# Layer 0 of a two-layer decoder trunk: queries and keys projected ahead of values and gates, and one head's attention laid over both projections of the next

## The chip, the cores and the metric

The kernel runs on one core of a Trainium2 chip. The metric is the device time of one execution in microseconds (us), and of several executions the median. The engines are named as in the profile: PE is TensorE's matmul side and PEld its weight loads, DVE is VectorE, ACT is ScalarE, POOL is GpSimd, and SP is the queue from which nearly all DMAs are issued.

## The reference

The model has two layers over 512 positions of width 2048 in float32. Layer 0 is differential attention with 8 heads, layer 1 is forgetting attention with 16 heads over keys and values that are projected once between the layers. Only the inside of layer 0 is changed:

```python
def diff_attention(h, w_in, w_out, ...):          # h = x * (1 + scale) + shift
    q, k, v, g = jnp.split(h @ w_in, 4, axis=-1)  # q, k: 8 heads x 2 x 128; v, g: 8 heads x 256
    ...
    sc = einsum('bqhcd,bkhcd->bhcqk', qb, k) + bias      # two score maps c per head, causal, ALiBi
    p = softmax(sc)
    a = p[:, :, 0] - lam * p[:, :, 1]
    o = einsum('bhqk,bkhe->bqhe', a, v)
    o = rms_norm(o, subln_g) * (1.0 - lam_init) * silu(g)
    return o @ w_out
```

The shift, scale and gate of both layers and of the shared keys and values are products of one vector (`silu(c)`) with large weight matrices (`w_mod`, `kv_w_mod`).

## The kernel before, in words

Every float32 product is made of three fp32r matmuls (function `products`, lines L173, L174, L175): each operand is split into a high part (a cast on ACT) and a low part (a subtraction on DVE). 512 positions are four blocks of 128; the width is 16 blocks of 128.

A projection is a `group`: four accumulator banks, 8 weight tiles ("subs") of 256 rows by 512 columns, and for each sub one burst for each bank. A burst is 2 x 3 matmuls of 128x512, so that a group is 32 bursts and 192 matmuls. The weight tiles come through `WeightStream`: a load on SP's queue (`wst`, four buffers), a cast on ACT (`whi`, L93) and a subtraction on DVE (`wlo`, L94), made two subs ahead of their use. The order of the weight tiles is written out once, in `ws.order`.

Head h of layer 0 has two groups. `vg[h]` projects its values and gates (the activations are the stationary operand; in the trace `acc<-whi,hh`), `qk[h]` its two queries and two keys (the weights are stationary; `acc<-hh,whi`). After its last burst a bank is evacuated: `evac_vg` splits the values and makes the gate, `evac_qk` splits a query or a key (L656, L657, L168, L169). The first two heads are projected mostly in the stage before, the last bank of their keys in a small group `kk`.

Attention of a head is a list of pieces, and after each burst (`tick`) one piece is popped and issued. For the four blocks i of positions and the two score maps there are `score` (three matmuls into `sc`, a DVE instruction that adds the bias and takes the minimum, L699, the exponential on ACT, L703, and DVE instructions that combine the two maps), `turn` (transposes into the one `tr` bank, L720, then a split into `ah`, `al`), `values` (products into `o`; after every second block `norm`, the RMS norm: squares on ACT, L749, a reciprocal root of 12 small DVE instructions, L750 and L246 to L255, and two multiplications with the gate, L753) and `store` (two transposes of the result, L767, which wait for L753, and a scaled copy into `ogT`, L769). `None` is a burst without a piece. `drain()` issues all pieces that are left.

Beside the bursts runs `background`: the products of `silu(c)` with `w_mod` and `kv_w_mod`, 256 steps of one DVE instruction (L384 or L386, `macc<-ms`) each, with a 512 KB load (`ms`, two buffers) for every two steps, and one short PE, DVE and DMA sequence after each sixteen steps (`mod_row`, L406 to L409). The argument `bg` of a group says in which bursts a step is taken: `k % 2` gives 16 steps in a group, `k % 3 > 0` gives 21. After the last head the out-projection takes a step in every burst until the steps are used up.

The order before: `kk`, `vg[2]` beside the attention of head 0, `qk[2]` beside that of head 1, and for h = 3 to 7 first `vg[h]` beside the attention of head h-1, then `qk[h]` beside no attention. In `qk[7]`, `split_og` (through `early`) also splits the finished heads' results into the operands of the out-projection, 14 casts on ACT and 14 subtractions on DVE. The attention of head 7 runs beside the first group of the out-projection. Instructions of an engine run in the order in which they stand; that order is made from the order of the program by a scheduler that may move independent instructions past each other.

Of the kernel before, what the change touches and what calls it, by code (L numbers as in the profile page):

```python
# [20 lines left out]
A_HEADS = 8  # L21
# [88 lines left out]
def tile_yoco(  # L110
# [147 lines left out]
    ws = WeightStream(nc, wpool)  # L258
    vg = [Job(a_w_in, [(4096 + 256 * h, 256), (6144 + 256 * h, 256)]) for h in range(A_HEADS)]
    qk = [Job(a_w_in, [(256 * h, 256), (2048 + 256 * h, 256)]) for h in range(A_HEADS)]  # L260

    first = {h: (Job(a_w_in, [(256 * h, 256), (2048 + 256 * h, 128)]), vg[h]) for h in range(2)}
# [16 lines left out]
                ws.add(j, s)  # L279
    ws.add_job(kk)  # L280
    for h in range(2, A_HEADS):
        ws.add_job(vg[h])
        ws.add_job(qk[h])
    for j in [o[1] for o in oA] + vj + kj + bj + [o[1] for o in oB]:
        ws.add_job(j)

    pieces = []
# [18 lines left out]
    def group(job, natural, evac, banks=range(4), bg=0, before_sub=None, after_sub=None, hold=0, after_held=None):  # L306


        acc = {b: acc_bank() for b in banks}
        w = job.width  # L310
        count = 0
        ns = KT // 2

        def burst(s, b, hi, lo):
            nonlocal count
            for kk in range(2):
                kt = 2 * s + kk
                bs = slice(b * P, (b + 1) * P)
                start, stop = kt == 0, kt == KT - 1
                if natural:  # L320
                    products(acc[b][:, :w], (Hh[kt][:, bs], Hl[kt][:, bs]), (hi[kk][:, :w], lo[kk][:, :w]), start, stop)
                else:
                    products(acc[b], (hi[kk][:, bs], lo[kk][:, bs]), (Hh[kt], Hl[kt]), start, stop)
            if s == ns - 1:
                evac(b, acc[b])
            tick(bg(count) if callable(bg) else bg)
            count += 1

        for s in range(ns - hold):
# [86 lines left out]
    part = {}  # L416
    with tc.tile_pool(name="start", bufs=2, reuse_waits="tile") as sp, tc.manual_schedule(engines={ET.DVE}):
# [110 lines left out]
        acc = {}  # L528
# [43 lines left out]
        def turn():  # L572
            lower()
            columns()
            while sum(sets[at["set"] - 1]) <= at["kt"]:
                sums()
                columns()
            turned.append((at["kt"], turn_x(at["kt"])))
            at["kt"] += 1
# [70 lines left out]
    def evac_qk(h):  # L650
        def fn(b, acc):
            name = ("q0", "q1", "k0", "k1")[b]
            hi = ap.tile([P, T], F32R, name=name + "h", tag=name + "h")
            lo = ap.tile([P, T], F32R, name=name + "l", tag=name + "l")
            if b < 2:
                S.activation(hi, acc, AF.Copy, scale=QS)  # L656
                V.scalar_tensor_tensor(lo, acc, QS, hi.bitcast(F32), op0=ALU.mult, op1=ALU.subtract)  # L657
            else:
                split(hi, lo, acc)
            cur[h, name] = (hi, lo)  # L660
        return fn

    def evac_vg(h):
        def fn(b, acc):
            if b == 0:
                cur[h, "v"] = (
                    ap.tile([P, TB, 256], F32R, name="vh", tag="vh"),
                    ap.tile([P, TB, 256], F32R, name="vl", tag="vl"),
                )
                cur[h, "sg"] = ap.tile([P, TB, 256], F32, name="sg", tag="sg")  # L670
            vh, vl = cur[h, "v"]
            split(vh[:, b, :], vl[:, b, :], acc[:, 0:256])
            th = ap.tile([P, 256], F32, name="th", tag="th", bufs=2)
            S.activation(th, acc[:, 256:512], AF.Tanh, scale=0.5)
            V.scalar_tensor_tensor(cur[h, "sg"][:, b, :], th, 1.0, acc[:, 256:512], op0=ALU.add, op1=ALU.mult)
        return fn

    def attention_a(h, lead=3, late=()):
        st = {}
        slope = 2.0 ** (-8.0 * (h + 1) / A_HEADS)  # L680

# [77 lines left out]
        def store(i):  # L759
# [11 lines left out]
                    )  # L771
            return fn

        return [
            *[None] * lead, score(0, 0), *late[0:1], score(0, 1), *late[1:2], score(1, 0), *late[2:3], score(1, 1), *late[3:4],
            turn(0), score(2, 0), values(0), turn(1), score(2, 1), values(1), score(3, 0), turn(2), score(3, 1), None,
# [3 lines left out]
    def drain():  # L780
        while pieces:
            tick(0)

    def first_qk(h):
        return [lambda b=b: evac_qk(h)(b, part[h][4 + b]) for b in (0, 2, 1)]

    def first_vg(h, src):
        return [lambda b=b: evac_vg(h)(b, src[b]) for b in range(4)]

    load_parameters()  # L790
    raw = {}

    def keep(key, acc):
        raw[key] = kpool.tile([P, T], F32, name="raw", tag="K")
        S.copy(raw[key], acc)
# [6 lines left out]
    def split_og(kts):  # L802
        for kt in kts:
            new_h(kt)
            split(Hh[kt], Hl[kt], ogT[kt])
# [2 lines left out]
    drain()  # L808
    pieces.append(lambda_columns)
    pieces.extend(attention_a(0, 2))  # L810
    group(vg[2], True, lambda b, acc: keep(b, acc), bg=lambda k: k % 2)
    drain()
    for h in range(2, A_HEADS):
        if h == 2:
            pieces.extend(first_qk(1))
            pieces.append(lambda: evac_qk(1)(3, raw["k1"]))
            pieces.extend(attention_a(1, 2, first_vg(1, part[1])))
        else:
            late = first_vg(2, raw) if h == 3 else ()
            pieces.extend(attention_a(h - 1, 3, late))  # L820
            group(vg[h], True, evac_vg(h), bg=lambda k: k % 2)
            drain()

        def early(s):
            if s >= 1:
                split_og((2 * s - 2, 2 * s - 1))

        def evac(b, acc, h=h):
            if b == 0:
                drain()  # L830
            evac_qk(h)(b, acc)

        group(qk[h], False, evac, bg=lambda k: k % 3 > 0, after_sub=early if h == A_HEADS - 1 else None)
    def ktile(name):
        return kpool.tile([P, T], F32, name=name, tag="K")

# [118 lines left out]
    npool, n, nstats = zp  # L955
# [81 lines left out]
    acc = [acc_bank() for _ in range(TB)]  # L1037
# [34 lines left out]
    for g in range(4):  # L1072
        if g == 2:
# [3 lines left out]
            after_sub=(lambda s: build_h((2 * s - 2, 2 * s - 1), ab["b"]) if s >= 1 else None) if g == 3 else None,  # L1077
# [221 lines left out]
```

## Time and profile before

| | |
|---|---|
| median of 3 runs | 2016.12 us (2012.25 to 2016.65) |
| the profiled execution's own time | 2017.03 us |
| its span, from the first to the last instruction | 2015.2 us |
| PE busy | 1966.7 us |
| DVE busy | 1334.4 us |
| ACT busy | 722.3 us |
| mean granted TensorE clock | 0.995 |

The page gives busy time by engine, the share of each engine in 40 slices, DMA queues, the chain of work that ended last, and groups of instructions. Behind it are views that answer for a stretch of time: busy time by engine and stretch ("windows"), instructions in order of time ("timeline"), and who waited for whom ("waits"). In the windows a row is the stretch in us, its length, then for PE, PEld, DVE, ACT and POOL the busy time and the number of instructions, then the granted clock, the busy share of the DMA engines and GB/s.

In the profiled execution the groups that the change touches stand at these times: `vg[2]` 222.0 to 278.8, `qk[2]` to 333.4, `vg[3]` to 388.3, `qk[3]` to 432.9, `vg[4]` to 486.8, `qk[4]` to 530.8, `vg[5]` to 587.2, `qk[5]` to 631.2, `vg[6]` to 685.9, `qk[6]` to 730.4, `vg[7]` to 784.3, `qk[7]` to 829.1, and then the out-projection.

### The profile page before, as it was taken

The numbers are of one execution on the slowest core, as the hardware profiler recorded it, in microseconds if no ns is written. First come the engines' busy times: TensorE is split into PE (matmuls) and PEld (weight loads), VectorE is DVE, ScalarE is ACT, GpSimd is POOL, SyncE is SP. The second block draws the span as 40 slices with busy tenths as digits, with TensorE's granted clock in tenths as the row PEclk, the third lists the DMA queues.
The fourth block names the chain that finished last, engine by engine and source line by source line (L and its number), as shares of the span: only waits on it lengthen the run. The fifth ranks groups of instructions, "written<-read, shape, count | busy, mean of one in ns | idle before, by whom it ended". The sixth has DMA issues, their size and how long they took to land.

```text
span 2015.2 us, 25053 instructions
## 1 busy us (share of the span) xinstructions
PE 1966.7 (98%) x9115; PEld 1624.6 (81%) x9115; DVE 1334.4 (66%) x2435; ACT 722.3 (36%) x1230; POOL 2.2 (0%) x10
## 2 busy tenths in 40 slices
PE   5999999999999999999999999999999999999997
PEld 4888878888878888888878877888888888888885
DVE  7887878777667677753575666645455555576678
ACT  2423444433333334432273222224333333453232
POOL 0000000000000000000000000000000000000000
PEclk8999999999999999999999999999999999999998
DMA  9995755574556565552344878844233323333754
GB/s 342 346 314 149 238 174 162 166 222 156 190 166 210 160 225 178 162 165 94 115 144 135 268 252 260 259 123 129 90 104 95 104 90 104 95 117 93 259 191 177
DMA packets 263095, 353.79 MB, mean 176 GB/s; under 512 B 18022, under 2 KB 162556, under 8 KB 262204
## 3 DMA queue, kind: packets, MB, share of 16 engines
q1 hardware_dynamic: 260592, 347.99, 53.7%
q10 hardware_dynamic: 2380, 4.21, 0.6%
q8 instruction: 71, 1.16, 0.2%
q14 instruction: 52, 0.43, 0.1%
HBM read 339.47 MB, written 12.66 MB: 175 GB/s over the span
## 4 chain that ended last, share of the span: by engine, by line
PE 77%; DVE 10%; DMA 10%; issue 2%; ACT 1%; SPq 1%; DVEq 0%; ACTq 0%
PE acc L173 22%; PE acc L175 22%; PE acc L174 22%; DMA ms<-in_w_mod_dram 7%; DVE macc L386 3%; DVE wlo L94 2%; PE sc L173 2%; PE sc L174 2%; PE sc L175 1%; DMA ms<-in_kv_w_mod_dram 1%; PE o L175 1%; PE o L174 1%; PE o L173 1%; PE tr L1163 1%; DMA sms<-in_w_mod_dram 1%
## 5 line engine op out<-in xcount | busy, mean ns | idle before, releaser
L93 ACT CAST whi<-wst 128x1024 fp32r<-128x1024 f32 (+2 forms) x339 | 349.5, 1032 | 672.9 <-PE acc L175 281.6
L94 DVE TENSOR_TENSOR wlo<-wst,whi 128x1024 fp32r<-128x1024 f32 (+2 forms) x339 | 404.4, 1195 | 268.1 <-ACT whi L93 263.9
L173 PE MATMUL acc<-whi,hh 128*128 128x512 f32 x1252 | 492.6, 397 | 0.9 <-ACT hh L933 0.8
L174 PE MATMUL acc<-wlo,hh 128*128 128x512 f32 x1252 | 489.7, 391 | 2.6 <-DVE wlo L94 2.6
L175 PE MATMUL acc<-whi,hl 128*128 128x512 f32 x1252 | 488.1, 390 | 0.0
L173 PE MATMUL acc<-hh,whi 128*128 128x512 f32 x1184 | 468.5, 396 | 1.3 <-ACT vt L977 0.9
L175 PE MATMUL acc<-hh,wlo 128*128 128x512 f32 x1184 | 462.3, 390 | 2.0 <-DVE wlo L94 2.0
L174 PE MATMUL acc<-hl,whi 128*128 128x512 f32 x1184 | 461.7, 390 | 0.0
L386 DVE SCALAR_TENSOR_TENSOR macc<-ms,cact,macc 128x512 f32<-128x512 f32 x360 | 269.9, 750 | 128.4 <-DMA ms<-in_w_mod_dram 95.6
L175 PEld LDWEIGHTS acc<-whi,hl 128*128 128x128 f32 x1252 | 235.3, 188 | 50.8 <-DVE hl L934 0.3
L174 PEld LDWEIGHTS acc<-wlo,hh 128*128 128x128 f32 x1252 | 235.6, 188 | 47.8 <-DVE wlo L94 4.3
L173 PEld LDWEIGHTS acc<-whi,hh 128*128 128x128 f32 x1252 | 235.7, 188 | 46.8 <-ACT hh L933 1.2
L175 PEld LDWEIGHTS acc<-hh,wlo 128*128 128x128 f32 x1184 | 222.3, 188 | 52.2 <-DVE wlo L94 4.2
L173 PEld LDWEIGHTS acc<-hh,whi 128*128 128x128 f32 x1184 | 222.5, 188 | 45.7 <-ACT vt L977 1.7
L174 PEld LDWEIGHTS acc<-hl,whi 128*128 128x128 f32 x1184 | 222.6, 188 | 41.1
L476 DVE SCALAR_TENSOR_TENSOR sacc<-sms,cact,sacc 128x512 f32<-128x512 f32 (+1 forms) x127 | 89.5, 705 | 4.8 <-DMA sms<-in_w_mod_dram 1.2
L1152 ACT ACTIVATE eb<-eb,mnb 128x128 f32<-128x128 f32 (+1 forms) x64 | 36.1, 563 | 96.4 <-DVE mnb L1149 95.2
L703 ACT ACTIVATE e<-e,mn 128x128 f32<-128x128 f32 (+3 forms) x64 | 36.0, 563 | 89.5 <-DVE mn L699 88.7
L1149 DVE CUSTOM_DVE_ANT_0 eb<-sc,biasb 128x128 f32<-128x128 f32 (+1 forms) x64 | 31.3, 490 | 52.7 <-PE sc L175 52.7
L1167 DVE TENSOR_TENSOR pTl<-tr,pTh 128x128 fp32r<-128x128 f32 (+1 forms) x64 | 31.2, 487 | 26.5 <-ACT pTh L1166 26.2
L1166 ACT CAST pTh<-tr 128x128 fp32r<-128x128 f32 (+1 forms) x64 | 27.2, 424 | 43.6 <-PE tr L1163 43.1
L769 ACT ACTIVATE ogT<-tr,subg 128x128 f32<-128x128 f32 x64 | 20.0, 364 | 56.4 <-PE tr L767 56.4
(251 smaller groups left out, 1739.2 us busy)
## 6 DMA issues: line engine op xcount, KB each, us to landing
wst<-in_a_w_in_dram SPq DMA_DIRECT2D x240, 256.0 KB
ms<-in_w_mod_dram SPq DMA_DIRECT2D x64, 512.0 KB
ms<-in_kv_w_mod_dram SPq DMA_DIRECT2D x64, 512.0 KB
wst<-in_kv_w_dram SPq DMA_DIRECT2D x64, 512.0 KB
ms<-in_w_mod_dram SPq DMA_DIRECT2D x128, 256.0 KB
wst<-in_b_w_in_dram SPq DMA_DIRECT2D x128, 256.0 KB
sms<-in_w_mod_dram SPq DMA_DIRECT2D x56, 512.0 KB
wst<-in_b_w_out_dram SPq DMA_DIRECT2D x48, 512.0 KB
```

The source lines that it names most:

```text
L93: self.nc.scalar.copy(hi[:, :, :w], st[:, :, :w])
L94: self.nc.vector.tensor_tensor(lo[:, :, :w], st[:, :, :w], hi[:, :, :w].bitcast(F32), op=ALU.subtract)
L173: PE.matmul(dst, lhs[0], rhs[0], start=start, stop=False)
L174: PE.matmul(dst, lhs[0], rhs[1], start=False, stop=False)
L175: PE.matmul(dst, lhs[1], rhs[0], start=False, stop=stop)
L386: V.scalar_tensor_tensor(acc, w, cact[:, kt : kt + 1], acc, op0=ALU.mult, op1=ALU.add)
L476: V.scalar_tensor_tensor(acc, w, sc, acc, op0=ALU.mult, op1=ALU.add)
L703: S.activation(e[:, :w], e[:, :w], AF.Exp, bias=mn, scale=-1.0, accum_out=rs)
L1149: V.tensor_tensor_reduce(out=e[:, :w], in0=sc[:, :w], in1=bias[:, :w], scale=-1.0, scalar=3.0e38, op0=ALU.add, op1=ALU.min, accum_out=mn)
L1152: S.activation(e[:, :w], e[:, :w], AF.Exp, bias=mn, scale=-1.0, accum_out=rs)
L1166: S.copy(pTh[:, 0 : i + 1, ts], src)
L1167: V.tensor_tensor(pTl[:, 0 : i + 1, ts], src, pTh[:, 0 : i + 1, ts].bitcast(F32), op=ALU.subtract)
```

## The change

`qk[h]` comes ahead of `vg[h]`, in the order of the weight tiles and in the order of the groups. The attention of heads 2 to 6 is cut into two lists: `first` (all scores, three of four `turn`s, two of four `values`, 22 places behind four empty ones) runs beside `qk[h]` of the next head, and `rest` (two `values`, the last `turn`, the four `store`s) beside `vg[h]`. The attention of head 0 now runs beside `qk[2]`, which takes no background steps; that of head 1 beside `vg[2]`, with 16. From head 3 on both groups take 21 steps. `qk[2]` is copied out of its banks (`raw`) and split later, beside `qk[3]`. The splitting of finished results (`early`) moves from `qk[7]` to `vg[7]`.

```diff
     for h in range(2, A_HEADS):
+        ws.add_job(qk[h])
         ws.add_job(vg[h])
-        ws.add_job(qk[h])
...
-    def attention_a(h, lead=3, late=()):
+    def attention_a(h, lead=3, late=(), spread=False):
...
+        if spread:
+            first = [
+                score(0, 0), None, score(0, 1), None, score(1, 0), None, score(1, 1), None, turn(0), None, score(2, 0), values(0),
+                None, turn(1), score(2, 1), None, values(1), score(3, 0), None, turn(2), None, score(3, 1),
+            ]
+            rest = [values(2), None, store(0), None, store(1), None, turn(3), None, None, values(3), *[None] * 9, store(2), None, store(3)]
+            return first, rest
         return [
...
-    group(vg[2], True, lambda b, acc: keep(b, acc), bg=lambda k: k % 2)
+    group(qk[2], False, lambda b, acc: keep(("qk", b), acc))
     drain()
-    for h in range(2, A_HEADS):
-        if h == 2:
-            pieces.extend(first_qk(1))
-            pieces.append(lambda: evac_qk(1)(3, raw["k1"]))
-            pieces.extend(attention_a(1, 2, first_vg(1, part[1])))
-        else:
-            late = first_vg(2, raw) if h == 3 else ()
-            pieces.extend(attention_a(h - 1, 3, late))
-            group(vg[h], True, evac_vg(h), bg=lambda k: k % 2)
-            drain()
+    pieces.extend(first_qk(1))
+    pieces.append(lambda: evac_qk(1)(3, raw["k1"]))
+    pieces.extend(attention_a(1, 2, first_vg(1, part[1])))
...
+    group(vg[2], True, keep_vg, bg=lambda k: k % 2)
+    for h in range(3, A_HEADS):
+        first_steps, rest = attention_a(h - 1, spread=True)
+        if h == 3:
+            pieces.extend(lambda b=b: evac_qk(2)(b, raw["qk", b]) for b in range(4))
+            late = first_vg(2, raw)
+            for n in range(4):
+                first_steps[2 * n + 1] = late[n]
+        else:
+            pieces.extend([None] * 4)
+        pieces.extend(first_steps)
...
-        group(qk[h], False, evac, bg=lambda k: k % 3 > 0, after_sub=early if h == A_HEADS - 1 else None)
+        group(qk[h], False, evac, bg=lambda k: k % 3 > 0)
+        pieces.extend(rest)
...
+        group(vg[h], True, evac_rest, bg=lambda k: k % 3 > 0, after_sub=early if h == A_HEADS - 1 else None)
```

More of the change, by code (lines that the diff above doesn't have):

```diff
@@ L810, in tile_yoco, with keep_vg @@
     pieces.extend(attention_a(0, 2))
-    group(vg[2], True, lambda b, acc: keep(b, acc), bg=lambda k: k % 2)
+    group(qk[2], False, lambda b, acc: keep(("qk", b), acc))
     drain()
-    for h in range(2, A_HEADS):
-        if h == 2:
-            pieces.extend(first_qk(1))
-            pieces.append(lambda: evac_qk(1)(3, raw["k1"]))
-            pieces.extend(attention_a(1, 2, first_vg(1, part[1])))
-        else:
-            late = first_vg(2, raw) if h == 3 else ()
-            pieces.extend(attention_a(h - 1, 3, late))
-            group(vg[h], True, evac_vg(h), bg=lambda k: k % 2)
-            drain()
-        def early(s):
-            if s >= 1:
-                split_og((2 * s - 2, 2 * s - 1))
+    pieces.extend(first_qk(1))
+    pieces.append(lambda: evac_qk(1)(3, raw["k1"]))
+    pieces.extend(attention_a(1, 2, first_vg(1, part[1])))
+    def keep_vg(b, acc):
+        if b == 0:
+            drain()
+        keep(b, acc)
+    group(vg[2], True, keep_vg, bg=lambda k: k % 2)
[6 more added lines that the diff above has]
+                first_steps[2 * n + 1] = late[n]
+        else:
+            pieces.extend([None] * 4)
+        pieces.extend(first_steps)
         def evac(b, acc, h=h):
@@ L831, in evac, with evac_rest, early @@
             evac_qk(h)(b, acc)
-        group(qk[h], False, evac, bg=lambda k: k % 3 > 0, after_sub=early if h == A_HEADS - 1 else None)
+        group(qk[h], False, evac, bg=lambda k: k % 3 > 0)
+        pieces.extend(rest)
+        def evac_rest(b, acc, h=h):
+            if b == 0:
+                drain()
+            evac_vg(h)(b, acc)
+        def early(s):
+            if s >= 1:
+                split_og((2 * s - 2, 2 * s - 1))
+        group(vg[h], True, evac_rest, bg=lambda k: k % 3 > 0, after_sub=early if h == A_HEADS - 1 else None)
     def ktile(name):
```

## The prediction

> **What bounds the kernel now.** I read the page's busy times and chain first, then the busy time by stretch for the groups that the change touches, then who waited for whom on PE there, and last single instructions in order of time.
>
> ```profile
> PE 1966.7 (98%) x9115; PEld 1624.6 (81%) x9115; DVE 1334.4 (66%) x2435; ACT 722.3 (36%) x1230; POOL 2.2 (0%) x10
> PE 77%; DVE 10%; DMA 10%; issue 2%; ACT 1%; SPq 1%; DVEq 0%; ACTq 0%
> ```
>
> PE is busy nearly always, and 77% of the chain that ended last is its work. A change that leaves PE's work alone can win only where PE waits. The built order of the changed kernel has the same 8720 rows on PE as before, none added and none taken away; up to the end of `kk`, and from the middle of the out-projection's first group, their order is the same too. So the whole effect lies in the groups of heads 2 to 7:
>
> ```profile
> 222.00:278.80 56.80, 54.28 (x268) 44.91 (x267) 48.97 (x118) 27.26 (x63) 0.00 (x0) 1.00 0.70 221
> 278.80:333.40 54.60, 53.67 (x264) 44.75 (x263) 36.47 (x90) 22.70 (x52) 0.00 (x0) 1.00 0.53 163
> 333.40:388.30 54.90, 54.74 (x272) 45.14 (x270) 42.70 (x114) 24.45 (x58) 0.00 (x0) 1.00 0.47 150
> 388.30:432.90 44.60, 44.60 (x199) 36.87 (x198) 29.96 (x39) 12.59 (x18) 0.00 (x0) 1.00 0.67 206
> 432.90:486.80 53.90, 53.90 (x267) 45.11 (x266) 40.28 (x101) 22.84 (x53) 0.00 (x0) 1.00 0.51 162
> 486.80:530.80 44.00, 44.00 (x195) 36.42 (x194) 29.20 (x39) 11.68 (x16) 0.00 (x0) 1.00 0.73 229
> 530.80:587.20 56.40, 54.41 (x268) 45.02 (x267) 42.23 (x104) 23.73 (x54) 0.00 (x0) 1.00 0.55 177
> 587.20:631.20 44.00, 44.00 (x196) 36.41 (x195) 25.42 (x32) 11.51 (x16) 0.00 (x0) 1.00 0.61 193
> 631.20:685.90 54.70, 54.22 (x268) 45.04 (x267) 38.70 (x100) 23.46 (x54) 0.00 (x0) 1.00 0.50 156
> 685.90:730.40 44.50, 44.50 (x198) 36.80 (x197) 28.87 (x38) 12.14 (x17) 0.00 (x0) 1.00 0.61 196
> 730.40:784.30 53.90, 53.90 (x267) 45.13 (x266) 40.45 (x100) 23.23 (x53) 0.00 (x0) 1.00 0.54 171
> 784.30:829.10 44.80, 44.35 (x196) 36.40 (x196) 35.15 (x51) 19.76 (x30) 0.00 (x0) 1.00 0.71 229
> ```
>
> The twelve rows are `vg[2]`, `qk[2]`, `vg[3]`, `qk[3]` and so on to `qk[7]`. Length less PE busy is PE's idle time: 2.52, 0.93, 0.16, 0, 0, 0, 1.99, 0, 0.48, 0, 0 and 0.45, together 6.53 us of 607. A group with attention takes some 54 us, one without 44, and the idle time lies almost wholly in the groups with attention. Its owners:
>
> ```profile
> PE tr L767 <- DVE og L753: 4.4, 5, 1.3
> PE tr L767 <- DVE al L169: 0.9, 1, 0.9
> PE tr L720 <- DVE ss L750: 0.6, 1, 0.6
> PE acc L173 <- DVE sg L675: 0.4, 1, 0.4
> ```
>
> Eight waits, longest 1.3 us, and five of them are the `store` transposes that come before `norm` is through. One of them in full, on DVE and then on PE:
>
> ```profile
> 573.64 0.17 DVE L750 TENSOR_SCALAR ss<-ss 128x2 f32<-128x2 f32 x1 [1.24 <-ACT o L749]
> ...
> 575.54 0.75 DVE L386 SCALAR_TENSOR_TENSOR macc<-ms,cact,macc 128x512 f32<-128x512 f32 x1 [0.53 <-DMA ms<-in_kv_w_mod_dram]
> ...
> 579.91 0.88 DVE L753 SCALAR_TENSOR_TENSOR og<-og,rstd,sg 128x256 f32<-128x256 f32 x2
> ```
>
> ```profile
> 580.54 0.41 PE L767 MATMUL tr<-ident,og 128*128 128x128 f32 x2 [1.08 <-DVE og L753]
> ```
>
> The norm's small instructions queue on DVE behind background steps, one of which waits for its load: 7.2 us from L750 to the end of L753 (579.91 + 0.88 - 573.64), of which the norm's own work is a fraction.
>
> **What a wait costs.** Undisturbed matmuls start 0.227 us apart and are shown 0.39 long:
>
> ```profile
> 490.89 0.39 PE L173 MATMUL acc<-hh,whi 128*128 128x512 f32 x1
> 491.12 0.39 PE L174 MATMUL acc<-hl,whi 128*128 128x512 f32 x1
> 491.34 0.39 PE L175 MATMUL acc<-hh,wlo 128*128 128x512 f32 x1
> ```
>
> So a wait that stops the stream costs its idle time and 0.39 - 0.227 = 0.16 us more. With eight of them the waits cost 6.53 + 1.3 = 7.8 us. That is all that there is to win. PE busy cannot show this, since its bars overlap. The Trainium skill, Perfetto Trace Analysis, section "Identifying the Most-Contended Engine", makes the same objection to matmul busy time and would read the share of weight loads instead. By that rule, with the 45.11 of 53.9 of `vg[4]` and the 36.42 of 44.0 of `qk[4]` as clean shares, the disturbed groups would hold about 9.5 us instead of 7.8, and the sum below would come to about -6.5. I keep the waits, whose owners the trace names.
>
> **The change, part by part.** Distances are counted in projection matmuls in the built order of each kernel, at 0.227 us.
>
> *Heads 2 to 6, attention over two groups.* From the second score of a block to its `turn` there were 18 matmuls (4.1 us) for block 0 and 2, and there are 36 and 30 (8.2 and 6.8 us). From `values(1)` to the first `store` there were 36 (8.2 us), and there are 84 (19 us). From `values(3)` to `store(2)` there were 30 to 37 (7 to 8 us), and there are 60 (13.6 us), against a chain of some 9 us from the products to the end of L753. The 3.08 us of idle time in `vg[3]` to `qk[7]` should go, with four or five tails of 0.16.
>
> What could come in their place is set by DVE. Its load by kind:
>
> ```profile
> L386 DVE SCALAR_TENSOR_TENSOR macc<-ms,cact,macc 128x512 f32<-128x512 f32 x16 | 12.0, 749 | 2.1 <-DMA ms<-in_kv_w_mod_dram 1.9
> L94 DVE TENSOR_TENSOR wlo<-wst,whi 128x1024 fp32r<-128x1024 f32 x8 | 9.8, 1221 | 4.7 <-ACT whi L93 4.7
> ```
>
> ```profile
> L386 DVE SCALAR_TENSOR_TENSOR macc<-ms,cact,macc 128x512 f32<-128x512 f32 x21 | 15.8, 751 | 7.8 <-DMA ms<-in_kv_w_mod_dram 7.3
> ```
>
> The first two rows are `vg[4]`, the third is `qk[4]`. In `vg[4]` 40.28 - 12.0 - 9.8 = 18.5 us are attention, evacuation and a `mod_row`; in `qk[4]` 29.20 - 15.8 - 9.8 = 3.6 us are the latter two; so attention is about 15 us, of which I put 11 into `first` (all scores, three `turn`s, one `norm`) and 4 into `rest`. A `qk` group after then holds 29.2 + 11 = 40 us of DVE work in about 50 us (80%), a `vg` group 15.8 + 9.8 + 3.6 + 4 = 33 in 48 (69%). The five steps more per head are 5 x 0.75 = 3.7 us of that and would cost nothing, being taken from the end. `first` also stands behind steps that wait for loads, which were 7.3 us in `qk[4]` and should be fewer where the group is longer. For scale: `vg[2]` before ran DVE at 48.97 of 56.8 (86%) and idled PE 2.52 us, `vg[4]` and `vg[7]` at 75% idled nothing, all at the tighter spacing. I take 0.1 us a group, 1.0 in all; the bounds are 0 and 2.52 for each of the ten.
>
> *Head 0 beside `qk[2]` without background.* The `store`s stand 36 and 38 matmuls behind their `values`, as before (36 and 37); what goes is DVE work:
>
> ```profile
> L386 DVE SCALAR_TENSOR_TENSOR macc<-ms,cact,macc 128x512 f32<-128x512 f32 x27 | 20.2, 749 | 2.9 <-DMA ms<-in_w_mod_dram 2.6
> ```
>
> That is `vg[2]`: 48.97 - 20.2 = 29 us of DVE work remain in 55. Of 2.52 us of idle time I leave 0.4; the bounds are 0 and the 0.93 of `qk[2]`, which had 36.47 us.
>
> *Head 1 beside `vg[2]`.* Spacing is the same as before beside `qk[2]`, and so are the steps, 15 there and 16 now:
>
> ```profile
> L386 DVE SCALAR_TENSOR_TENSOR macc<-ms,cact,macc 128x512 f32<-128x512 f32 x15 | 11.2, 746 | 1.7 <-DMA ms<-in_w_mod_dram 1.6
> ```
>
> I leave its 0.93 us; the bounds are 0 and 2.52.
>
> *The detour of `qk[2]` through `raw`.* Four more copies on ACT (0.6 us each, as the casts of 512 columns below) and four splits that move into `qk[3]`, 2.7 us of DVE work by the row of 0.69 us each; hidden beside 44 us of matmuls, and 2.7 us at most if the first score had to wait for all of them.
>
> *`early` in `vg[7]`.* From `qk[7]`:
>
> ```profile
> L169 DVE TENSOR_TENSOR hl<-ogT,hh 128x512 fp32r<-128x512 f32 x14 | 9.6, 686 | 3.2 <-PE acc L174 3.2
> L168 ACT CAST hh<-ogT 128x512 fp32r<-128x512 f32 x14 | 8.7, 620 | 21.9 <-PE acc L174 21.9
> ```
>
> DVE in `vg[7]` comes to 33 + 9.6 = 43 us in 48 (89%). Behind the waiting `hh` and `hl` stand only `rest` pieces, with 60 matmuls to spare, and weight tiles made two subs (11 us) ahead. I put 0.2 us, between 0 and 2.52.
>
> *Weights, SP and DMA.* The same loads in the other order. Four steps more are done before the out-projection, whose evacuation had the rest to finish: 0, or up to 3 us in its favour (4 x 0.75) that PE does not wait for now. POOL has no part.
>
> *Sum.* Idle time -2.52 + 0.4, -3.08 + 1.0, +0.2, and six or seven tails, -1.0: -5.0 us. Against the profiled execution (2017.03, its span and 1.8 us around it) that is 2012.0; the median of the runs lies 0.91 lower, so 2011.1 us.
>
> **Rivals.** *The waits come back elsewhere (0.36).* Eighty per cent on DVE in `qk` is nearer to the 86% of `vg[2]` than the groups that idled nothing; if each of the ten groups idles 0.3 to 0.8 us, 3 to 8 us come back, of 7.8 won less 1.3 left: the end lies between 2012.6 and 2017.6. For it speaks the row of `qk[4]` with 7.3 us of DVE waiting for loads, which attention now queues behind; against it that every distance on PE has grown.
>
> *DVE becomes the bound of the `qk` groups (0.09).* If attention or the waits for loads are 6 us larger there than I put them, DVE passes 90% of the group, and banks, scores and `wlo` come late together. It decides from the 86% of `vg[2]` on; at twice that group's 2.52 us in the five `qk` groups and once in the five `vg` groups, 38 us are lost against 6.5 won; at once in the `qk` groups alone, 12.6 less 6.5, so 2022 us. I price it at 2022.
>
> *A slow clock (0.02).* PE's clock fell in this trace when PE starved at the start:
>
> ```profile
> 34.00:39.00 5.00, 5.00 (x13) 3.88 (x13) 4.46 (x7) 1.33 (x2) 0.00 (x0) 0.54 1.09 388
> ```
>
> ```profile
> 37.28 0.63 PE L174 MATMUL o<-hl,whi 128*128 128x512 f32 x1
> 37.71 0.63 PE L175 MATMUL o<-hh,wlo 128*128 128x512 f32 x1
> ```
>
> Matmuls started 0.43 us apart there, 0.2 more than 0.227, and 13 in 5 us lost 2.6 us. One such stretch in each of five heads would be 13 us, less the 5 won: 2024 us. The Trainium skill, TensorE: Matmul & The Clock Gate, section "HAM oscillation — how this bites in real kernels", lets the clock fall after an idle gap of over about 3.4 us. The rows above show 1.00 in all twelve groups with no wait over 1.3 us, so the trace agrees and speaks against it.
>
> *The change does not do what it says (0.01).* A scheduler could move the pieces together again; the built order shows them apart.
>
> **How the numbers follow.** The forecast has 0.52: waits mostly gone, 2007.5 to 2012.1. 0.2% is 4.0 us, about what a measurement of this kernel can tell from no change, and the forecast lies just beyond it. So faster is 0.52, the same 0.37 (the first rival and the last), slower 0.11. The range goes from all 7.8 us won, less 0.8 for the spread of the runs, 2007.5, to 2016.5, which takes in most of the first rival and leaves out its worst and the slow cases.
>
> **What would show it.** Right: `vg` and `qk` groups of heads 4 to 6 both near 49 us, PE idle under 0.3 us in each, no wait of the `store` transposes for `og` there, DVE near 80% in `qk` and 69% in `vg`. Wrong: DVE above 86% in a `qk` group with waits of `tr`, `sc` or `acc` for it; or groups without idle time whose sum is still not below 98 us per head, which would mean that inserted pieces cost PE more than their matmuls.

## The result and the profile after

Over 15 runs each, the changed kernel has a median of 2010.79 us (2008.66 to 2016.58) and the kernel before 2015.13 us (2009.52 to 2021.51). The ratio is 0.998 with a 95% interval of 0.9971 to 0.9989, so the change makes the kernel faster by some 4 us (2.2 to 5.8). The forecast was 2011.1 us. Part of that nearness is luck: the difference forecast was 5.0 us, the difference of the medians is 4.3, and the median of the kernel before came out 1.0 us lower than in the three runs shown first.

The profiled execution of the changed kernel took 2009.60 us, with a span of 2007.8 us and a granted clock of 0.995. Its page, busy time by engine and the chain that ended last:

```profile
PE 1966.9 (98%) x9115; PEld 1626.8 (81%) x9115; DVE 1336.5 (67%) x2435; ACT 724.5 (36%) x1234; POOL 2.2 (0%) x10
PE 84%; DVE 7%; DMA 6%; issue 1%; SPq 1%; ACT 1%; DVEq 0%; ACTq 0%
```

The work of every engine is what it was (PE 1966.7 us before, 1966.9 now); only the share of the last chain that is PE's own grew from 77 to 84%. The windows of the changed kernel, one row for each group, in the order `qk[2]`, `vg[2]`, `qk[3]`, `vg[3]`, `qk[4]`, `vg[4]`, and, behind the gap, `qk[7]` and `vg[7]` (length, then PE, PEld, DVE, ACT and POOL busy, granted clock, DMA share, GB/s):

```profile
222.60:278.70 56.10, 53.47 (x263) 43.89 (x262) 48.32 (x118) 25.89 (x61) 0.00 (x0) 1.00 0.67 219
278.70:332.30 53.60, 53.60 (x264) 44.92 (x263) 27.21 (x75) 25.41 (x56) 0.00 (x0) 1.00 0.28 90
332.30:382.80 50.50, 50.00 (x237) 41.38 (x235) 38.67 (x92) 20.63 (x45) 0.00 (x0) 1.00 0.49 157
382.80:432.00 49.20, 49.20 (x233) 40.92 (x232) 32.83 (x56) 16.82 (x31) 0.00 (x0) 1.00 0.61 192
432.00:482.00 50.00, 50.00 (x235) 41.56 (x234) 39.64 (x89) 19.14 (x39) 0.00 (x0) 1.00 0.62 202
482.00:530.20 48.20, 48.20 (x229) 40.08 (x228) 31.73 (x55) 15.73 (x29) 0.00 (x0) 1.00 0.66 215
...
727.50:777.40 49.90, 49.90 (x235) 41.65 (x234) 41.23 (x91) 18.59 (x39) 0.00 (x0) 1.00 0.64 202
777.40:825.80 48.40, 48.40 (x230) 40.24 (x229) 40.06 (x68) 22.97 (x42) 0.00 (x0) 1.00 0.69 225
```

The twelve groups lasted 829.1 - 222.0 = 607.1 us before and last 825.8 - 222.6 = 603.2 us now: 3.9 us less, beside 4.3 us between the medians. From `vg[3]` on no group idles. What idle time is left is 56.10 - 53.47 = 2.63 us in `qk[2]` and 50.50 - 50.00 = 0.50 us at the head of `qk[3]`, where the last `store` of head 1 is late. Who waited on PE from 222 to 886 us (waits: total, how many, the longest):

```profile
PE tr L769 <- DVE og L755: 2.9, 3, 1.3
PE o L175 <- DVE al L169: 0.2, 1, 0.2
```

The first row are again `store` transposes that wait for `norm` (L769 and L755 are L767 and L753 of the kernel before), all of heads 0 and 1; the second is a product of head 0 that waits for a split. Four waits are left of eight. Idle time fell by 6.53 - 3.13 = 3.40 us and the tails by 4 x 0.16 = 0.64, together 4.0 us against the 3.9 measured in these two executions. How near the two come to the 4 us of the medians is in part luck of this pair: both kernels were profiled once more (below, as the kernel before again and the last two kernels side by side). From L237 (`tr<-lam`), six matmuls into the first group, to the first score of head 7, in the out-projection's first group, the kernel before took 608.4 and 606.7 us, the changed kernel 604.7 and 604.8. Between these marks that is 3.8 us for the first pair and 2.0 for the second.

The two profiled executions differ by more, 2017.03 - 2009.60 = 7.4 us. Most of the rest arises between 1143 and 1290 us, in layer 1, where the order of the instructions is the same in both: the waits are 5.2 us there before and 1.7 us after. The waits on PE there, in the kernel before and then in the changed one:

```profile
PE acc L174 <- DVE wlo L94: 2.3, 3, 1.0
PE acc L175 <- DVE wlo L94: 2.0, 4, 0.9
PE acc L173 <- ACT vt L977: 0.9, 2, 0.5
```

```profile
PE acc L175 <- DVE wlo L94: 1.1, 2, 0.7
PE acc L173 <- ACT vt L1006: 0.6, 1, 0.6
```

A pair of single profiles would therefore have shown a gain almost twice too large. The medians give the 4 us; the stretch that the change touches gives 3.8 and 2.0 in the two pairs of profiles.

### The profile page after: what moved, and what is told of

It reads as the page before. It is cut to its first block, busy times and chain, and to the rows that moved or that the text cites. A ratio compares the mean times of both kernels' runs of the same rounds, so it can differ in the third digit from the quotient of the medians.

```text
span 2007.8 us, 25027 instructions
## 1 busy us (share of the span) xinstructions
PE 1966.9 (98%) x9115; PEld 1626.8 (81%) x9115; DVE 1336.5 (67%) x2435; ACT 724.5 (36%) x1234; POOL 2.2 (0%) x10
## 4 chain that ended last, share of the span: by engine, by line
PE 84%; DVE 7%; DMA 6%; issue 1%; SPq 1%; ACT 1%; DVEq 0%; ACTq 0%
PE acc L173 24%; PE acc L175 24%; PE acc L174 24%; DMA ms<-in_w_mod_dram 5%; DVE wlo L94 2%; PE sc L173 2%; PE sc L174 2%; PE sc L175 2%; DVE macc L386 2%; PE o L175 1%; PE o L174 1%; PE o L173 1%; PE tr L1192 1%; SPq L449 0%; DVE z L1283 0%
## 5 line engine op out<-in xcount | busy, mean ns | idle before, releaser
L386 DVE SCALAR_TENSOR_TENSOR macc<-ms,cact,macc 128x512 f32<-128x512 f32 x360 | 270.0, 750 | 117.3 <-DMA ms<-in_w_mod_dram 90.2
L173 PEld LDWEIGHTS acc<-hh,whi 128*128 128x128 f32 x1184 | 222.6, 188 | 43.1 <-ACT vt L1006 1.0
L701 DVE CUSTOM_DVE_ANT_0 e<-sc,bias 128x128 f32<-128x128 f32 (+3 forms) x64 | 31.1, 486 | 16.2 <-PE sc L175 16.1
```

What stands on the lines that cost most here:

```text
L173: PE.matmul(dst, lhs[0], rhs[0], start=start, stop=False)
L386: V.scalar_tensor_tensor(acc, w, cact[:, kt : kt + 1], acc, op0=ALU.mult, op1=ALU.add)
L701: V.tensor_tensor_reduce(out=e[:, :w], in0=sc[:, :w], in1=st["bias"][:, (3 - i) * P :], scale=-1.0, scalar=3.0e38, op0=ALU.add, op1=ALU.mi ...
```

## The experiments

The theory was that the waits of the `store` transposes are gone because their distance on PE from the products that they need has grown while `norm` stays clear of the evacuation of the values. The rivals were the order of the groups in itself, the lighter DVE load of the groups, and a gain of the out-projection's beginning that comes from the background steps.

**The kernel before again.** The same kernel, to see how far two of its executions differ.

> The kernel before, once more with a profile. The two profiles so far differ by 7.4 us, of which 3.6 arise before 1143 us and 5 between 1143 and 1290 us, where the instructions of both stand in the same order. If that part is a difference from one execution to the next, the waits for wlo and vt in that stretch are another sum here than the 5.2 us of the first profile of this kernel, by 1 us or more; if it came from the change, they are 5.2 us again.

It took 2013.46 us. Between 1143 and 1290 us it shows waits of 1.7, 1.1 and 0.4 us, 3.2 in all, where the first profile has 5.2: that part of the difference between the two profiles belongs to the execution and not to the change. The changed kernel, run again below, has 4.4 us of waits there where its first profile has 1.7. From 222 to 900 us this run has the known waits, 3.6 us of `store` for `og` in four places, 0.9 us for `al` and 0.2 for `sg`: 4.7 us where the first profile has 6.3. So the stretch that the change touches varies from one execution to the next too, here by 1.7 us (608.4 and 606.7).

**The order alone.** The changed kernel with the attention of heads 2 to 6 kept together beside `qk`.

```diff
-        first_steps, rest = attention_a(h - 1, spread=True)
...
+            pieces.extend(attention_a(2, 0, first_vg(2, raw)))
         else:
-            pieces.extend([None] * 4)
-        pieces.extend(first_steps)
+            pieces.extend(attention_a(h - 1, 3))
...
-        pieces.extend(rest)
```

> The changed kernel, with the queries and keys still ahead of the values and gates and the same background rates, but the attention of heads 2 to 6 packed into the qk group as it was packed into the vg group before (store(2) some 30 matmuls behind values(3)). Theory (distance of the stores decides): PE idles again in the qk groups of heads 3 to 7, about 3 us together where the changed kernel idles 0 and the kernel before 3.1; of the gain of 4 us about 1 is left or none. Rival (the order of the two groups decides): those groups idle nothing and the time is that of the changed kernel, ratio 0.998.

Its median was 2018.03 us beside 2015.82 before, a ratio of 1.0016 (1.0005 to 1.0026): slower. Its waits on PE from 222 to 886 us, first two rows:

```profile
PE tr L769 <- DVE og L755: 6.0, 8, 1.2
PE tr L769 <- DVE al L169: 0.3, 1, 0.3
...
```

Five of those eight waits, 3.1 us, lie behind 340 us, in the groups where the changed kernel has none. So it is not the order of the groups that took them away. This kernel keeps the changed rates of the background, and that is a second difference from the kernel before; the next one takes it out.

**The order alone, at the old rates.** As the last, with 21, 16, 16 and 21 steps in `qk[2]`, `vg[2]`, `qk[h]` and `vg[h]`. From head 3 on the group with attention again takes 16 and the one without 21, as before.

```diff
-    group(qk[2], False, lambda b, acc: keep(("qk", b), acc))
+    group(qk[2], False, lambda b, acc: keep(("qk", b), acc), bg=lambda k: k % 3 > 0)
...
-        group(qk[h], False, evac, bg=lambda k: k % 3 > 0)
+        group(qk[h], False, evac, bg=lambda k: k % 2)
```

> The order of the groups alone, clean of the rates: qk[h] ahead of vg[h], the attention packed beside qk[h] with 16 steps, 21 beside vg[h], 21 beside qk[2], 16 beside vg[2], so 222 steps as before the change. The first run of the order alone had 21 steps beside the packed attention and was slower by 0.16%. Theory (the order in itself is worth nothing): PE idles about 3 us in the groups of heads 3 to 7 and the ratio to the kernel before is 0.9995 to 1.001. Rival (the order helps or harms by itself): 0.9985 or less, or 1.0015 or more.

Its median was 2015.93 us beside 2015.3, a ratio of 1.0001 (0.9993 to 1.001). The waits from 222 to 886 us:

```profile
PE tr L769 <- DVE og L755: 4.2, 5, 1.2
PE acc L173 <- DVE sg L675: 1.5, 2, 0.8
...
```

The order of the groups in itself is worth nothing that can be measured. The kernel with the raised rates came out some 3 us slower than this one, but the two intervals overlap, and its waits in these groups are of the same size; whether the rates cost anything there is not settled.

**The stores close together again.** The changed kernel with the last two `store`s at their old distance.

```diff
-            rest = [values(2), None, store(0), None, store(1), None, turn(3), None, None, values(3), *[None] * 9, store(2), None, store(3)]
+            rest = [values(2), None, store(0), None, store(1), None, turn(3), None, None, values(3), *[None] * 4, store(2), store(3)]
```

> The changed kernel with only the last two stores of heads 2 to 6 pulled forward: four empty places behind values(3) where there were nine, so 30 matmuls as before. Theory (distance): the wait of the store transposes for og comes back in the vg groups of heads 3 to 7, 0.3 to 1 us a group, 1.5 to 4 us together, and nowhere else. Rival (what helps is that DVE's work is spread evenly, 31 to 33 us of 48 in a vg group): no wait comes back, the time is that of the changed kernel.

Its median was 2014.05 us beside 2015.82, a ratio of 0.9993 (0.9984 to 1.0002). The waits from 388 to 830 us, where the changed kernel shows none:

```profile
PE tr L769 <- DVE og L755: 1.5, 3, 0.9
PE tr L769 <- DVE mrow L408: 0.3, 1, 0.3
```

All four stand at `store(2)`. Five bursts less between `values(3)` and `store(2)` give 1.8 us of waits back, with four tails 2.4 us of the gain of 4. The medians agree with that size, but the interval takes in no change from the kernel before and overlaps that of the changed kernel; the evidence is where the waits came back.

**The last stores alone.** The kernel before, its order kept, with only the last two `store`s of heads 3 to 6 moved back.

```diff
-            values(2), store(0), turn(3), store(1), values(3), None, None, None, None, store(2), store(3),
+            values(2), store(0), turn(3), store(1), values(3), *[None] * (9 if far else 4), store(2), *[None] * far, store(3),
...
-            drain()
+            if h == 3:
+                drain()
```

> The kernel before with only the last two stores of heads 3 to 6 moved back (nine empty places behind values(3) instead of four, so into the end of the vg group and the start of the qk group); values, first stores and norm stay where they were, unlike in the run that moved all four. Theory (distance, if the norm stays clear of the evacuation): the wait of 1.1 us at the end of vg[5] goes, nothing comes in the place of it, the waits of first stores (0.9 us in vg[5], 0.5 in vg[6]) and the 0.45 at the start of qk[7] stay: 1 to 1.5 us won, ratio 0.9993. Rival (any delay of stores collides with the evacuation, as in the run that moved all four): waits for sg or og of 1 us or more at the borders, ratio 1.000 or above.

Its median was 2012.35 us beside 2015.14, a ratio of 0.9988 (0.9979 to 0.9997), which takes in the 0.9993 expected. From 388 to 829 us one wait is left of what were 2.92 us:

```profile
PE tr L767 <- DVE al L169: 0.7, 1, 0.7
```

Here no group changes its place and no attention is spread over a second projection. By the medians distance alone wins 2.4 us (0.6 to 4.2) of the 4.0 that the change wins. The traces show less of it. The wait of the moved `store` in `vg[5]`, 1.1 us at 580 us in the first profile of the kernel before and 1.2 us in the repeated one, is gone. Of the other three waits, which belong to no `store` that was moved, the 0.5 us at 665 us was missing in the repeated profile of the kernel before as well, so its absence here shows nothing. From 222 to 388 us, which the edit does not touch, this execution waits 4.1 us where the two of the kernel before waited 3.5 and 2.5. So some 1.2 us and a tail are traced to the distance; the rest of the 2.4 is not.

**All stores moved back, order kept.** The kernel before, with the `turn` and `values` of block 3, and so the second `norm`, later as well.

```diff
+                values(2), None, turn(3), None, store(0), None, store(1), None, values(3), *[None] * 9, store(2), None, store(3),
```

> The kernel before, its order of groups and its rates, with the four stores of heads 3 to 6 moved back alone: store(0) nine pieces behind values(1) instead of six, store(2) ten behind values(3) instead of five, so that the last two fall into the qk group. Theory (distance): the idle time of vg[4] to qk[7], 2.9 us before, falls under 0.6, and the time falls by 2.5 to 3.5 us, ratio 0.9985, most of what the whole change won in those heads. Rival (order, or DVE's load, decides): the waits stay, 2 to 3 us, ratio 1.000.

This theory missed. The median was 2022.23 us beside 2015.82, a ratio of 1.004 (1.0024 to 1.0055). The waits from 222 to 886 us:

```profile
PE tr L767 <- DVE og L753: 5.7, 4, 2.9
PE acc L173 <- DVE sg L675: 1.8, 2, 1.6
PE tr L767 <- ACT ogT L769: 0.7, 1, 0.7
PE tr L406 <- ACT ogT L769: 0.7, 1, 0.7
PE tr L767 <- DVE al L169: 0.5, 1, 0.5
```

With `values(3)` later, `norm` falls into the end of the `vg` group. There DVE also has the evacuation of that same group, and a gate buffer (`sg`, L675) can't be written before `norm` has read it. Both `store`s of head 6 then come late, at the border of two groups; the timeline of PE and the windows:

```profile
787.09 0.66 PE L767 MATMUL tr<-ident,og 128*128 128x128 f32 x2 [2.87 <-DVE og L753]
788.46 0.69 PE L767 MATMUL tr<-ident,og 128*128 128x128 f32 x2 [0.71 <-ACT ogT L769]
...
790.88 0.63 PE L174 MATMUL acc<-hl,whi 128*128 128x512 f32 x1
791.31 0.63 PE L175 MATMUL acc<-hh,wlo 128*128 128x512 f32 x1
```

```profile
787.00:791.00 4.00, 2.48 (x7) 1.52 (x8) 3.22 (x6) 1.82 (x6) 0.00 (x0) 0.50 0.38 128
791.00:794.00 3.00, 3.00 (x9) 2.35 (x8) 1.84 (x3) 0.60 (x2) 0.00 (x0) 0.53 0.64 208
```

The waits sum to 5.7 + 1.8 + 0.7 + 0.7 + 0.5 = 9.4 us, 2.8 of them ahead of 333 us in groups that the edit does not touch, and behind the long one the granted clock falls to 0.5, with matmuls 0.43 us apart. So distance is not to be had at every place: in the changed kernel the second `norm` runs in the middle of a `vg` group and finds DVE free and `sg` not yet wanted. That is what laying a head over two groups adds to the distance. A single kernel with the old order and that place for `norm` was not run.

**Short background steps at the start.** The changed kernel, with DVE's work in the first 48 steps of the background and their loads cut down.

```diff
+            if nk > 1 and i < 3:
+                nc.sync.dma_start(t[:, 0, 0:64], src[nk * r * P : nk * r * P + P, col : col + 64])
+                loaded[k] = t
+                return
...
+                if nk > 1 and i < 3:
+                    V.tensor_scalar(acc[:, 0:16], t[:, 0, 0:16], cact[:, 0:1], None, op0=ALU.mult)
-                if kt == 0:
+                elif kt == 0:
```

> The changed kernel, with the first 48 background steps (three sixteenths of the background, those that run up to head 3) cut to 16 columns and to loads of 32 KB; what is left out is the sum for three quarters of layer 0's gate. It tells apart why head 0's stores still wait 2.6 us beside qk[2], which takes no steps in the program but shows 48 us of DVE work, steps among it, in the changed kernel's trace. Load on DVE (my prediction's reason, with the steps gone that it believed gone): the waits between 222 and 333 us fall from 2.6 us to 0.4 or less, DVE there from 48 to about 30 us. The chain alone (norm's instructions and 36 matmuls of distance are too tight in themselves): 2 us or more stay.

One run took 2007.41 us. The windows of `qk[2]` and `vg[2]`:

```profile
222.10:278.00 55.90, 55.90 (x277) 46.53 (x276) 34.20 (x104) 28.00 (x63) 0.00 (x0) 1.00 0.33 107
278.00:332.00 54.00, 53.51 (x266) 44.55 (x264) 29.42 (x85) 26.68 (x59) 0.00 (x0) 1.00 0.24 79
```

DVE's work in `qk[2]` falls from 48.32 to 34.20 us, and PE's 2.63 us of idle time with it to nothing. The only wait left from 222 to 345 us is one of 0.5 us for `og`, at 330 us. So the background steps do set the waits of head 0. The edit takes away their work on DVE and most of their loads at once, so it does not tell the one from the other: in the changed kernel DVE also stands idle for 4.5 us there because steps wait for `ms`.

**Lower rates.** The changed kernel with 16 steps instead of 21 in each of `vg[3]` to `vg[7]`.

```diff
-        group(vg[h], True, evac_rest, bg=lambda k: k % 3 > 0, after_sub=early if h == A_HEADS - 1 else None)
+        group(vg[h], True, evac_rest, bg=lambda k: k % 2, after_sub=early if h == A_HEADS - 1 else None)
```

> The changed kernel with the old rate of background steps beside vg[3] to vg[7]: 16 steps instead of 21, as before the change. Theory (distance): PE idles nothing in the groups of heads 3 to 7, as with 21; the 25 steps that are left over go to the out-projection and its evacuation, which can cost 0 to 3 us there; ratio 0.998 to 0.9995. Rival (the even rates won it): 1 us or more of idle time comes back in the qk or vg groups of heads 3 to 7.

Every theory missed it. The median was 2026.53 us beside 2015.14, a ratio of 1.0056 (1.0044 to 1.0069), 11 us slower than the kernel before. The waits on PE from 222 to 900 us, the windows from 886 us on, and two rows of DVE's timeline:

```profile
PE tr L929 <- DVE mrow L408: 3.8, 1, 3.8
PE tr L406 <- DVE mrow L408: 3.1, 1, 3.1
PE tr L769 <- DVE og L755: 2.9, 3, 1.5
...
```

```profile
886.00:893.00 7.00, 1.70 (x4) 0.87 (x5) 2.33 (x7) 0.00 (x0) 0.00 (x0) 0.54 0.26 88
893.00:897.00 4.00, 4.00 (x11) 3.12 (x11) 4.00 (x8) 0.00 (x0) 0.00 (x0) 0.53 0.72 122
```

```profile
880.48 1.54 DVE L386 SCALAR_TENSOR_TENSOR macc<-ms,cact,macc 128x512 f32<-128x512 f32 x2 [0.47 <-DMA ms<-in_w_mod_dram]
...
890.45 0.68 DVE L408 SCALAR_TENSOR_TENSOR mrow<-tr,mrow 1x512 f32<-1x512 f32 x1 [4.23 <-DMA mrow<-in_b_mod_dram]
```

In heads 3 to 7 only 0.8 us of PE's time is idle, so the lower load does no harm there. But 25 more steps are left for the out-projection, whose first evacuation asks for all of them, and their end comes too late for it. The steps themselves are through at 882.0 us (the first of the two rows). What PE waits for are the closing sequences (`mod_row`) of the last two sums: both use the one `mrow` buffer, so the second must first store the row of the one ahead and then load its own bias, and DVE stands idle for 4.2 us until that load has landed (the second row). PE, whose next instructions need the `tr` bank that L408 reads, waits 3.1 and 3.8 us for it and 1.2 us for the evacuation behind it, and then runs at half its clock. In the changed kernel the last step is through before 828 us and PE has no wait of this kind. The higher rates of the change do not win anything in the groups that they are in. They pay for the 21 steps that `qk[2]` no longer takes.

**All stores moved back in the changed kernel.** What the change does for heads 2 to 6 is done for heads 0 and 1 too: their last two `store`s run in the next group, between the scores of the next head.

```diff
+        if far is not None:
+            gap = [None] * (2 - len(far))
+            main = [
+                *[None] * lead, score(0, 0), *late[0:1], score(0, 1), *far[0:1], *late[1:2], score(1, 0), *late[2:3], *far[1:2],
...
+                score(3, 1), None, values(2), None, turn(3), None, *gap, store(0), None, store(1), *gap[:1], values(3),
+            ]
+            return main, [store(2), store(3)]
...
-    pieces.extend(attention_a(0, 2))
+    main, tail = attention_a(0, 2, far=())
+    pieces.extend(main)
     group(qk[2], False, lambda b, acc: keep(("qk", b), acc))
-    drain()
...
-    pieces.extend(attention_a(1, 2, first_vg(1, part[1])))
+    main, tail = attention_a(1, 2, first_vg(1, part[1]), far=tail)
+    pieces.extend(main)
...
+            first_steps[4:4] = tail[1:]
+            first_steps[1:1] = tail[:1]
```

> The changed kernel, and the stores of heads 0 and 1 moved back too: store(0) nine or ten pieces behind values(1), the last two stores into the next group. Theory (distance): the 3.1 us that PE still idles between 222 and 383 us fall under 0.8; with the tails 2.5 to 3 us are won on the changed kernel, ratio to the kernel before about 0.9965. Rival (these waits are there because DVE is busy for 48 of 56 us in that group): 2 to 3 us of idle time stay, at the stores or at the next transposes, and the ratio stays at 0.998.

Its median was 2010.1 us beside 2015.82, a ratio of 0.997 (0.9958 to 0.9983). PE waits nowhere between 222 and 1000 us. The windows of `qk[2]` and `vg[2]`:

```profile
222.80:278.70 55.90, 55.90 (x274) 46.68 (x274) 46.93 (x113) 25.68 (x57) 0.00 (x0) 1.00 0.71 229
278.70:332.00 53.30, 53.30 (x264) 44.46 (x263) 28.17 (x81) 26.00 (x60) 0.00 (x0) 1.00 0.25 80
```

DVE is as full in `qk[2]` as in the changed kernel (46.93 us beside 48.32), and yet nothing idles. The load makes `norm` late, and the distance decides whether anyone waits for it.

**The last two kernels side by side.** The same two kernels once more, on one chip.

> The changed kernel once more, as the other side of that comparison: ratio to the kernel before about 0.998, PE idle 2.6 us beside qk[2], 0.5 at the start of qk[3], 0 from there to the out-projection.

> The version with the stores of heads 0 and 1 moved back as well, once more, now beside the changed kernel on the same chip. It had no wait of PE between 222 and 1000 us. Theory: it keeps 2.5 to 3 us on the changed kernel, ratio to the kernel before 0.9965 to 0.997. If its first result was luck: equal to the changed kernel within 1 us.

The changed kernel had a median of 2011.16 us, a ratio of 0.998 (0.9971 to 0.9988) to the kernel before; the one with all stores moved back had 2009.48 us and 0.9969 (0.9959 to 0.9979). Between 222 and 886 us the first waits 3.1 us and the second 0.3. The second is the fastest of the kernels that do all the work, some 2 us below the changed one; the intervals of the two still overlap, so the size of that step is less certain than its cause. Between the same two instructions as above, its two profiles lasted 601.3 and 601.6 us, where the changed kernel took 604.7 and 604.8: 3.2 to 3.4 us less.

## Why the prediction was right, and where it was not

**What can be won.** Waits and their tails were the right unit: 3.40 us of idle time less and four tails less are 4.0 us, and the stretch became 3.9 us shorter. The limit of 7.8 us was that of one execution. The repeated run of the kernel before has six waits of 4.7 us in all, so there some 5.7 us could be won, tails included. The Trainium skill, Perfetto Trace Analysis, section "Identifying the Most-Contended Engine", read through the shares of weight loads, would have led to 6.5 us; the first pair of traces shows 4.0.

**Heads 2 to 6: right, and better than forecast.** Of 3.08 us 1.0 was to stay, and nothing stayed. DVE came out at 79% (39.64 of 50.00, `qk[4]`) where 80% was forecast, and at 66% (31.73 of 48.20, `vg[4]`) where it was 69%. That the order of the groups does not carry the gain is shown by the two kernels that have it alone (1.0016 and 1.0001); that the distance does is shown at the `store`s themselves, where waits come back when it is taken away and one goes when it alone is added. That the kernel with all four stores moved in the old order lost time shows that distance by itself is not enough. One of the prediction's signs of being wrong did turn up: `qk` and `vg` without idle time, but with 98.2, 98.7, 98.6 and 98.3 us for heads 4 to 7, where it asked for less than 98. The mark was set too low, by the one clean head of the kernel before: less their idle time, the same heads took 97.9, 98.4, 98.7 and 98.3 us there.

**Head 0 beside `qk[2]`: the mis-sized term.** The forecast left 0.4 us of 2.52, and 2.63 us were measured, 2.2 us more. The step that failed is "29 us of DVE work remain": the group takes no background steps in the program, but it holds them in the built order. In the changed kernel, grouped by form, from 222.6 to 278.7 us:

```profile
L386 DVE SCALAR_TENSOR_TENSOR macc<-ms,cact,macc 128x512 f32<-128x512 f32 x27 | 20.2, 749 | 4.8 <-DMA ms<-in_w_mod_dram 4.5
```

The same 27 steps and 20.2 us stand here as in `vg[2]` before. The scheduler moves steps of later groups ahead, since they depend on nothing but their loads. The prediction's own row of `vg[2]` pointed to it: 27 steps in a group that takes 16. That a `qk[2]` without this load would have brought the gain is shown by the short steps (34.20 us of DVE work, nothing idle). What a loaded DVE does to a chain of small instructions is seen in the timeline, DVE and then PE:

```profile
248.31 0.16 DVE L752 TENSOR_SCALAR ss<-ss 128x2 f32<-128x2 f32 x1
248.38 0.74 DVE L386 SCALAR_TENSOR_TENSOR macc<-ms,cact,macc 128x512 f32<-128x512 f32 x1
249.04 0.16 DVE L246 TENSOR_SCALAR rs_t<-ss 128x2 int32<-128x2 int32 x1
...
256.97 0.87 DVE L755 SCALAR_TENSOR_TENSOR og<-og,rstd,sg 128x256 f32<-128x256 f32 x2
```

```profile
257.59 0.41 PE L769 MATMUL tr<-ident,og 128*128 128x128 f32 x2 [1.26 <-DVE og L755]
```

From L752 to the end of L755 go 256.97 + 0.87 - 248.31 = 9.5 us, for 13 small instructions of some 0.16 us each and the pair of L755, 0.87 us together. Between them stand wide instructions of 0.5 to 1.2 us, background or not.

**Head 1 beside `vg[2]`: wrong to its favour.** The forecast left 0.93 us and took the 15 or 16 steps for given. They had been done in `qk[2]` (no row of L386 lies between 278.7 and 332.3 us), DVE had 27.21 us of work in 53.60, and nothing idles. The last `store`, at the head of `qk[3]`, waits 0.50 us, so 0.43 us were won here.

**`early` in `vg[7]`: small, as forecast.** DVE holds 40.06 of 48.40 us, 83% and not 89%, and PE idles nothing where 0.2 us were put.

**The sum.** Head 0 +0.11 instead of -2.12, head 1 -0.43 instead of 0, heads 2 to 6 -3.08 instead of -2.08, `early` 0 instead of +0.2, tails -0.64 instead of -1.0: -4.0 instead of -5.0. The two larger misses offset each other in part.

**The background at nothing.** The term "0, or up to 3 us in its favour" held only because rates were raised. It priced steps as DVE work beside matmuls. With 16 steps in `vg`, PE stands still for 3.1 + 3.8 + 1.2 = 8.1 us where the out-projection's first evacuation asks for the end of the background, and that kernel lies some 15 us above the changed one (2026.53 against 0.998 of 2015.14). This place was missing in the prediction.

**The rivals.** The waits did not come back from DVE's load in `qk`, and DVE did not become the bound: from `qk[4]` on no group idles, with DVE at 79 to 83% in the `qk` groups. The clock stayed at 1.00 in all twelve groups. Long waits and a fallen clock do occur in a neighbour of this kernel, the one with all stores moved back in the old order: the waits where `norm` falls into the evacuation of the values, the fallen clock behind them.

## What to carry to other kernels

Where an in-order engine is nearly always busy, list its waits with their owners, count how much of its own work lies between a result's producer and its consumer in the built order, and compare that with how long the chain takes among everything else queued on the helping engine; moving the consumer back can take the wait away at an unchanged load of that engine, as long as the chain does not slide into another burst of its work. Read where background work stands from the built order and not from the program, and ask where all that is left of it falls due. Compare medians, and more than one profile of each kernel, since between two executions of the kernel before the waits of a stretch that the change leaves alone differed by 2.0 us and the length of the stretch that it touches by 1.7.

## What was not expected of the hardware

The granted clock fell behind short waits. In the kernel with the order alone a single wait came ahead of it; PE's timeline and the window:

```profile
1178.18 0.50 PE L174 MATMUL acc<-wlo,hh 128*128 128x512 f32 x1 [1.83 <-DVE wlo L94]
...
1179.37 0.63 PE L175 MATMUL acc<-whi,hl 128*128 128x512 f32 x1
1179.79 0.63 PE L173 MATMUL acc<-whi,hh 128*128 128x512 f32 x1
```

```profile
1178.00:1183.00 5.00, 4.82 (x14) 3.83 (x15) 3.44 (x6) 0.00 (x0) 0.00 (x0) 0.66 0.86 269
```

After 1.83 us of idling the matmuls ran at 0.23 us apart for 0.8 us more and then at 0.43 us for some 3 us. In the repeated kernel with all stores moved back a wait of 1.77 us at the same weight tile cost nothing of the kind; the window that begins with its end:

```profile
1170.00:1175.00 5.00, 4.99 (x22) 4.15 (x23) 3.31 (x5) 0.00 (x0) 0.00 (x0) 1.00 0.84 277
```

In the kernel with the lower rates a wait of 2.06 us, longer than the 1.83, ended at 1235.6 us, and there the clock stayed as well:

```profile
1235.00:1240.00 5.00, 4.42 (x19) 3.68 (x20) 3.83 (x5) 0.00 (x0) 0.00 (x0) 1.00 0.76 251
```

The Trainium skill, TensorE: Matmul & The Clock Gate, section "HAM oscillation — how this bites in real kernels", puts the fall behind an idle gap of over about 3.4 us; the measured 1.83 us differs, and the measurement decides. The length of the one gap does not settle it, since the longer one of 2.06 us passed; what else does stays open.
